# Two stages of a decoder layer in seven products instead of eight: the query projection of cross-attention, and the first two column blocks of the feed-forward

## The chip, the cores and the metric

The kernel runs on one core of a Trainium2 chip. Its time is the device time of one execution in microseconds; a figure for a kernel is the median of several executions. The engines are named as in the profile: PE (TensorE matmul) with its weight loads (PEld), DVE (VectorE), ACT (ScalarE), POOL (GpSimd) and SP (SyncE, which issues the DMAs).

## The reference, cut to what matters

One decoder layer over 1024 tokens of width 1024: a token mixer (stick-breaking attention and a Mamba-2 mixer side by side), cross-attention into 256 memory tokens with 4 heads, and a SwiGLU feed-forward with 2816 hidden units. Each part takes a normalised input and adds its normalised output to the stream. The change touches the second and the third part:

```python
x = x + rms_norm(merged @ w_mix_out[l], g_post_mix[l])
h = rms_norm(x, g_pre_xa[l])
mem_n = rms_norm(mem, g_mem[l])
x = x + rms_norm(memory_cross_attention(h, mem_n, w_xq[l], w_xkv[l], w_xo[l]), g_post_xa[l])
h = rms_norm(x, g_pre_ffn[l])
x = x + rms_norm(swiglu(h, w_gu[l], w_down[l]), g_post_ffn[l])
```

Inside, `q = h @ w_xq`, then scores, softmax and `o @ w_xo`; the feed-forward is `(silu(h @ w_gate) * (h @ w_up)) @ w_down`. All numbers are fp32.

## The kernel before, in words

**Products in two parts.** An fp32 matrix is held as a high part (rounded to fp32r, a form that PE multiplies fast) and a low part, the rest. `hi_sb` makes the high part as a copy on ACT or POOL, `lo_of` (L101) the low part as a subtraction, mostly on DVE. A product is then three matmuls per block of 128 rows of the inner dimension (`mm3`, L104 to L106, or `acc3`, L215 to L217): high by high, high by low, low by high. A matmul of one weight block of 128x128 with 512 columns is written 128x512 in the profile.

**Seven products instead of eight.** A product of two matrices that are cut into 2x2 blocks needs eight block products, or seven after Winograd and Strassen, if sums and differences of blocks are made first. Here the inner dimension (1024) is cut in two, the tokens are cut in two halves of 512, and two column blocks of the weight form a pair. `winograd_weights` (L173) makes the sums s1 to s4 of the weight's quarters on POOL (L183 to L186) and splits all seven; `winograd_pair` (L222) does the seven products of 12 matmuls each. On the other side stand the blocks b11, b21 (first half of the tokens) and b22, and the combinations t1 to t4 of the halves. The plain way takes 8 x 12 matmuls for a pair.

**The order of the stages.** `out_proj` (L1398) multiplies by an output matrix, chunk by chunk of 128 tokens (48 matmuls each, four chunks a call), then adds the normalised result to the stream (L1414 square and sum on ACT, `rstd_of` on POOL, L1416 and L1417 on DVE), stores it, and calls `pre_norm` (L157), which normalises the stream for the next part (L160 ACT, L161 DVE), transposes it (8 transposes, L165) and splits it into high (L166, ACT) and low (L167, DVE). After both halves (`hx`), the query projection follows: `proj` (L1443) for 8 column blocks and 2 halves, each 24 matmuls. The first two blocks' products with the first half stand ahead (`pre`, L1467): they need only tokens that are finished, while the last chunk is still being normalised. `wq_load` (L1434) loads a weight block and splits it.

Then come the scores (`soft`, L1506), softmax, transposes of prob (`turn_`, L1520) and the mix with the values (`mix`). The output matrix of cross-attention is loaded and split by `big_weight` (L1329, 8 slices of 512 KB through two raw buffers); its buffers lie on the right side of the memory, where qT and part of prob were. A second pair of `out_proj` calls follows.

**The feed-forward's beginning.** The first two of its 22 column blocks (a gate block and an up block each) are done the plain way by `standard` (192 matmuls). Beside them `combos` forms t1, t2 and t3 from the split blocks: `whole` (L1601) adds the high and the low part again, L1610 to L1614 subtract, `split` makes high and low; t4 follows after both (L1626). Only then come the 20 pairs of `strassen`.

**What sets the order.** A scheduler places the instructions of each engine in one fixed order when the kernel is built; an engine then waits at each instruction for what it needs. `behind(marks[n])` makes some loads and splits come after a named instruction. Pools hold a set number of buffers, and a new tile waits for the last reader of the buffer that it takes over.

## Time and profile before

| | us |
|---|---|
| median of 3 runs | 2554.7 (2552.59 to 2555.76) |
| profiled execution | 2557.21 |
| its span | 2555.4 |
| PE busy in the span | 2475.9 (97%) |
| DVE, ACT, POOL busy | 1772.8, 1133.7, 853.9 |
| query projection | 1638.4 to 1730.0 in the span |
| attention's scores, softmax and mix | 1730.0 to 1792.9 |
| second output projection | 1792.9 to 1887.9 |
| plain feed-forward blocks | 1887.9 to 1934.3 |
| the 20 pairs | 1934.3 to 2324.3 |

A row of a timeline reads: start in us from the span's start, length in us, engine, line, operation, output and inputs by the program's names, shape, number of instructions; in brackets the idle time before it and what ended it. Where rows overlap on PE, the matmuls run through the array one behind the other, and the distance of two starts is what one costs. The mean granted clock of PE was 0.992 of full speed in this execution.

### The profile page before, as it was taken

Reading aid. Unit: us, or ns where it says so; the run is one execution under the profiler, and the core shown is the slowest. Engines: PE = TensorE matmul, PEld = TensorE weight load, DVE = VectorE, ACT = ScalarE, POOL = GpSimd, SP = SyncE. Lnnn points to the kernel's source line nnn. Section 1 sums busy time; section 2 is a strip of 40 time slices with the busy share of each in tenths; the row PEclk is TensorE's granted clock in tenths of the full one; section 3 lists DMA queues with packets and bytes.
Section 4 is the critical chain, followed back from the end, with each engine's and each line's share of the span. In section 5 each row is a group of like instructions: output and inputs, shape, how many; then the busy total and the mean of one; then the engine's idle time right before and its main releaser. Section 6 shows DMA issues by size and latency. Waiting matters only on the chain. (4 is left out here: it accounts for less than half of the span.)

```text
span 2555.4 us, 33383 instructions
## 1 busy us (share of the span) xinstructions
PE 2475.9 (97%) x12378; PEld 2033.6 (80%) x12378; DVE 1772.8 (69%) x2093; ACT 1133.7 (44%) x2023; POOL 853.9 (33%) x650
## 2 busy tenths in 40 slices
PE   7999999999999999999999999999999999999998
PEld 5788888887888878777777788887787888888876
DVE  7665777767578787688888664316459666666997
ACT  5333455555456665566554213215233333334343
POOL 3221544443121211256656040101113333323772
PEclk9999999999999999999999999999999999999999
DMA  7431443332543434365332662311232232224232
GB/s 246 152 116 55 138 149 99 99 112 90 153 112 87 120 99 104 100 207 168 107 106 65 203 209 83 124 50 34 99 116 66 83 91 75 90 91 165 99 132 99
DMA packets 255275, 293.51 MB, mean 115 GB/s; under 512 B 17023, under 2 KB 175240, under 8 KB 254986
## 3 DMA queue, kind: packets, MB, share of 16 engines
q1 hardware_dynamic: 255114, 291.40, 36.6%
q8 instruction: 97, 1.59, 0.3%
q14 instruction: 64, 0.52, 0.1%
HBM read 200.10 MB, written 74.45 MB: 107 GB/s over the span
## 5 line engine op out<-in xcount | busy, mean ns | idle before, releaser
L875 DVE TENSOR_TENSOR_SCAN n<-n,mask 128x128 f32<-128x128 f32 (+7 forms) x128 | 181.7, 1445 | 23.4 <-ACT n L874 22.2
L101 DVE TENSOR_TENSOR sw<-sf,sw 128x512 fp32r<-128x512 f32 x150 | 120.9, 818 | 82.0 <-ACT sw L98 80.5
L892 ACT ACTIVATE wth<-tr,mone 128x512 fp32r<-128x512 f32 x192 | 110.2, 584 | 81.4 <-PE tr L889 80.6
L98 ACT ACTIVATE sw<-sf 128x512 fp32r<-128x512 f32 x150 | 92.1, 626 | 113.0 <-PE mm L217 97.8
L183 POOL TENSOR_TENSOR sf<-wr,wr 128x512 f32<-128x512 f32 x38 | 59.4, 1563 | 233.4 <-DMA wr<-in_w_gu_dram 116.7
L893 DVE SCALAR_TENSOR_TENSOR wtl<-tr,wth 128x512 fp32r<-128x512 f32 x192 | 99.3, 544 | 53.9 <-ACT wth L892 53.8
L98 ACT ACTIVATE sw<-wr 128x512 fp32r<-128x512 f32 x113 | 71.2, 631 | 126.2 <-PE mm L217 125.6
L217 PE MATMUL mm<-h,sw 128*128 128x512 f32 x320 | 125.0, 392 | 1.8 <-DVE sw L101 1.8
L215 PE MATMUL mm<-h,sw 128*128 128x512 f32 x320 | 122.6, 391 | 2.9 <-ACT h L98 2.3
L216 PE MATMUL mm<-h,sw 128*128 128x512 f32 x320 | 125.3, 391 | 0.0
L101 DVE TENSOR_TENSOR sw<-wr,sw 128x512 fp32r<-128x512 f32 x113 | 106.6, 945 | 21.1 <-ACT sw L98 21.0
L669 DVE SCALAR_TENSOR_TENSOR b<-b,prmT,b 128x1023 f32<-128x1023 f32 (+2 forms) x72 | 109.6, 1522 | 15.1 <-ACT b L667 14.5
L94 POOL TENSOR_SCALAR v<-va 128x512 fp32r<-128x512 f32 x16 | 20.6, 1289 | 278.2 <-PE av L902 164.0
L874 ACT ACTIVATE n<-sc 128x512 f32<-128x512 f32 (+1 forms) x192 | 88.6, 494 | 45.5 <-PE tr L889 28.8
L152 POOL TENSOR_SCALAR rstd<-ms 128x1 f32<-128x1 f32 x74 | 28.1, 379 | 237.1 <-ACT x L1414 110.3
L104 PE MATMUL mm<-oth,bw 128*128 128x512 f32 x256 | 103.6, 405 | 3.6 <-DVE a L1214 3.6
L104 PE MATMUL p<-bw,h 128*128 128x512 f32 x256 | 98.7, 391 | 3.3 <-DVE x L1416 2.4
L105 PE MATMUL mm<-otl,bw 128*128 128x512 f32 x256 | 100.5, 393 | 0.0
L106 PE MATMUL mm<-oth,bw 128*128 128x512 f32 x256 | 100.4, 392 | 0.0
L106 PE MATMUL p<-bw,h 128*128 128x512 f32 x256 | 100.1, 392 | 0.0
L105 PE MATMUL p<-bw,h 128*128 128x512 f32 x256 | 99.9, 390 | 0.0
L185 POOL TENSOR_TENSOR sf<-wr 128x512 f32<-128x512 f32 x38 | 63.0, 1657 | 105.4 <-DVE sw L101 105.4
(616 smaller groups left out, 8044.0 us busy)
## 6 DMA issues: line engine op xcount, KB each, us to landing
wr<-in_w_gu_dram SPq DMA_DIRECT2D x80, 256.0 KB
wr<-in_w_in_dram SPq DMA_DIRECT2D x36, 512.0 KB
zr<-in_w_in_dram SPq DMA_DIRECT2D x28, 512.0 KB
gu_d<-t SPq DMA_DIRECT2D x44, 256.0 KB
wraw<-in_w_in_dram SPq DMA_DIRECT2D x20, 512.0 KB
zs_d<-zo SPq DMA_DIRECT2D x32, 256.0 KB
xs_d<-b SPq DMA_DIRECT2D x32, 256.0 KB
kl<-gt SPq DMA_DIRECT2D x64, 128.0 KB
```

Source lines behind the costliest of these rows:

```text
L98: A.activation(o, i, AF.Copy)
L101: eng.tensor_tensor(o, i, hi.bitcast(F32), ALU.subtract)
L104: first = T.matmul(ps, sh, mh, start=start, stop=False)
L105: T.matmul(ps, sh, ml, start=False, stop=False)
L106: T.matmul(ps, sl, mh, start=False, stop=stop)
L215: T.matmul(ps, w[0][:, k, :], bh, start=first and k == 0, stop=False, skip_group_check=True)
L216: T.matmul(ps, w[0][:, k, :], bl, start=False, stop=False, skip_group_check=True)
L217: ins = T.matmul(ps, w[1][:, k, :], bh, start=False, stop=last and k == 3, skip_group_check=True)
L669: V.scalar_tensor_tensor(acc[:, sh:], y[:, :S - sh], cw(3 - sh, f), acc[:, sh:], ALU.mult, ALU.add)
L875: V.tensor_tensor_scan(nt[:, 0:L][:, ::-1], nt[:, 0:L][:, ::-1], mask[:, S - L:][:, ::-1], 1.0, ALU.mult, ALU.max)
L892: A.activation(wh[:, t0 * P:], pt[:, t0 * P:], AF.Identity, bias=mone)
L893: V.scalar_tensor_tensor(wl[:, t0 * P:], pt[:, t0 * P:], -1.0, wh[:, t0 * P:].bitcast(F32), ALU.add, ALU.subtract)
```

## The change

- The query projection is done in four pairs of seven products. Two pairs are interleaved in a new function `two_pairs`, the other two go through `winograd_weights` and `winograd_pair`. The same `two_pairs` does the first two column blocks of the feed-forward; `standard`, `combos`, `whole` and the t4 loop are gone.
- The combinations are formed in fp32 straight from the transposes, before a split. In the first half each chunk is also copied to fp32 tiles (x11 and x21, two more ACT copies); in the second half `pre_norm` forms b22, t1 and the fp32 block of t2 chunk by chunk (L1462, L1464 to L1466 in the new file). `other_blocks` then makes t3 and t4 (four subtractions of 128x1024, L1484 and L1487) and splits t2, t3 and t4 (six high parts on ACT, six low parts on DVE).
- Ahead of the last chunk stand three products (`lead_products`, 36 matmuls) in place of two `proj` calls (48), with weights from `lead_weights`.
- In `two_pairs`, s1 is made on DVE (L1526), s2, s3 and s4 on POOL. The raw weights are loaded into tiles that are used later for other things: qT4 to qT7 in the query projection, fg and fw in the feed-forward.
- Memory: the values and the transposed keys take over the fp32 tiles; the pools of prob and of the softmax parts now lie where `big_weight`'s raw buffers and first slices come to lie, and qT lies beyond them. The keys' load is issued later. The reservation for software DMA is 256 instead of 1024.

The diff, cut to its core (the bodies of the removed functions stand above):

```diff
-    def pre_norm(psp, xt, yt, gbc, outs):
+    def pre_norm(psp, xt, yt, gbc, put):
 
         ms = mk(stats, [P, 1], F32, "ms")
         A.activation(yt, xt, AF.Square, scale=D ** -0.5, accum_out=ms)
         V.scalar_tensor_tensor(yt, xt, rstd_of(ms), gbc, ALU.mult, ALU.mult)
-        for kh, (hi, lo) in enumerate(outs):
-            pt = mk(psp, [P, 4, P], F32, "tr")
+        pts = []
+        for kh in range(2):
+            pts.append(mk(psp, [P, 4, P], F32, "tr"))
             for k in range(4):
-                T.transpose(pt[:, k, :], yt[:, (kh * 4 + k) * P:(kh * 4 + k + 1) * P], ident)
-            A.activation(hi, pt, AF.Copy)
-            V.tensor_tensor(lo, pt, hi.bitcast(F32), ALU.subtract)
+                T.transpose(pts[kh][:, k, :], yt[:, (kh * 4 + k) * P:(kh * 4 + k + 1) * P], ident)
+        put(pts, yt)
...
+        r0 = mk(rawp, [P, 4, 2, P], F32, tag)
+        r1 = mk(rawp, [P, 4, 2, P], F32, tag)
...
+            both[i] = mk(firstp if firstp is not None and i in (0, 3) else swp, [P, 2, 4, P], F32R, "sw")
...
     h2 = pool(px, "h2", 8)
-    wq = pool(px, "wq", 2)
+    xk = pool(px, "xk", 1)
+    ld = pool(px, "ld", 2)
     xt4 = ExitStack()
     t4 = pool(xt4, "t4x", 3)
+    psa = pool(px, "psa", 2, PSUM)
...
-    def wq_load(rawp, tag, src, rb=None, eng=None):
...
+    def fp32_blocks():
+
+        return [mk(xk, [P, 4, HALF], F32, f"xk{i}") for i in range(3)]
+
+    def first_half(hb, xf):
+        hb["b11"], hb["b21"] = quad(accp, "a8")
+
+        def at(cs):
+            def put(pts, yt):
+                for nm, pt in zip(("b11", "b21"), pts):
+                    hi, lo = [t[:, :, cs] for t in hb[nm]]
+                    A.activation(hi, pt, AF.Copy)
+                    V.tensor_tensor(lo, pt, hi.bitcast(F32), ALU.subtract)
+                for x, pt in zip(xf, pts):
+                    A.activation(x[:, :, cs], pt, AF.Copy)
+            return put
+        return at
+
+    def second_half(hb, xf):
+        hb["b22"], hb["t1"] = quad(h2, "h2")
+
+        def at(cs):
+            def put(pts, yt):
+                b22, t1 = [[t[:, :, cs] for t in hb[nm]] for nm in ("b22", "t1")]
+                x = yt[:, 0:HALF].rearrange("p (k t) -> p k t", t=P)
+                A.activation(b22[0], pts[1], AF.Copy)
+                V.tensor_tensor(x, pts[0], xf[0][:, :, cs], ALU.subtract)
+                A.activation(t1[0], x, AF.Copy)
+                V.tensor_tensor(b22[1], pts[1], b22[0].bitcast(F32), ALU.subtract)
+                V.tensor_tensor(xf[2][:, :, cs], pts[1], x, ALU.subtract)
+                V.tensor_tensor(t1[1], x, t1[0].bitcast(F32), ALU.subtract)
+            return put
+        return at
+
+    def other_blocks(hb, xf, tx):
+
+        hb["t2"], hb["t3"] = quad(h2, "h2")
+        hb["t4"] = tuple(mk(tx, [P, 4, HALF], F32R, "tx") for _ in range(2))
+        x11, x21, x2 = xf
+
+        def split(x, nm):
+            hi, lo = hb[nm]
+            for k in (0, 2):
+                hi_sb(hi[:, k:k + 2, :], x[:, k:k + 2, :], "a")
+                lo_of(lo[:, k:k + 2, :], x[:, k:k + 2, :], hi[:, k:k + 2, :])
+
+        split(x2, "t2")
+        for k in (0, 2):
+            V.tensor_tensor(x11[:, k:k + 2, :], x2[:, k:k + 2, :], x11[:, k:k + 2, :], ALU.subtract)
+        split(x11, "t3")
+        for k in (0, 2):
+            V.tensor_tensor(x21[:, k:k + 2, :], x21[:, k:k + 2, :], x2[:, k:k + 2, :], ALU.subtract)
+        split(x21, "t4")
+
+    def quarter_load(dst, w, kh, c0):
+        nc.sync.dma_start(dst.rearrange("p k b f -> p k (b f)"), w[kh * 512:(kh + 1) * 512, c0:c0 + 2 * P].rearrange("(k p) f -> p k f", p=P))
+
+    def split_weight(pl, tag, x):
+        o = mk(pl, [P, 2, 4, P], F32R, tag)
+        hi_sb(o[:, 0], x, "a")
+        lo_of(o[:, 1], x, o[:, 0])
+        return o[:, 0], o[:, 1]
+
+    def lead_weights(wbig, w):
+
+        raws = [mk(wbig, [P, 4, 2, P], F32, "wraw", 2) for _ in range(2)]
+        for kh in range(2):
+            quarter_load(raws[kh], w, kh, 0)
+        return [split_weight(pl, tag, raws[kh][:, :, p]) for pl, tag, kh, p in ((ld, "sw", 0, 0), (ld, "sw", 1, 0), (t4, "x4", 0, 1))]
+
+    def lead_products(hb, lead, pa, pb):
+        acc3(pa[0], lead[0], hb["b11"], True, False)
+        acc3(pb[0], lead[1], hb["b21"], True, True)
+        acc3(pa[1], lead[2], hb["b11"], True, False)
+
+    def two_pairs(hb, pa, pb, pc, raws, w, c1, sfp, swp, y, last, blocks):
+
+        (a11, a12), (a21, a22) = raws
+        for r, kh, c0 in ((a12, 1, 0), (a21, 0, c1), (a22, 1, c1), (a11, 0, 0)):
+            quarter_load(r, w, kh, c0)
+        acc3(pb[1], split_weight(swp, "sw", a12[:, :, 1]), hb["b21"], True, True)
+        for p in range(2):
+            A.activation(y[p][0][0], pa[p], AF.Copy)
+            V.tensor_tensor(y[p][0][0], y[p][0][0], pb[p], ALU.add)
+
+        def pick(r):
+            return [r[:, :, p] for p in range(2)]
+
+        def combined(eng, dst, x, z, op):
+            for o, i, j in zip(dst, x, z):
+                eng.tensor_tensor(o, i, j, op)
+            return dst
+
+        def rooms():
+            return [mk(sfp, [P, 4, P], F32, "sf") for _ in range(2)]
+
+        def weights(x):
+            return [split_weight(swp, "sw", t) for t in x]
+
+        def products(ps, ws, nm, start, stop, then):
+            for p in range(2):
+                acc3(ps[p], ws[p], hb[nm], start, stop)
+                then(p)
+
+        a11, a12, a21, a22 = [pick(r) for r in (a11, a12, a21, a22)]
+        s1 = combined(V, rooms(), a21, a22, ALU.add)
+        w1 = weights(s1)
+        s2 = combined(G, rooms(), s1, a11, ALU.subtract)
+        blocks()
+        w2 = weights(s2)
+        products(pc, w1, "t1", True, False, lambda p: A.activation(y[p][1][1], pc[p], AF.Copy))
+        w4 = weights(combined(G, a12, a12, s2, ALU.subtract))
+        products(pa, w2, "t2", False, False, lambda p: A.activation(y[p][0][1], pa[p], AF.Copy))
+        w3 = weights(combined(G, a21, a11, a21, ALU.subtract))
+        products(pc, w4, "b22", False, True, lambda p: V.tensor_tensor(y[p][0][1], y[p][0][1], pc[p], ALU.add))
+        w7 = weights(a22)
+        products(pa, w3, "t3", False, False, lambda p: V.tensor_tensor(y[p][1][1], y[p][1][1], pa[p], ALU.add))
+        products(pa, w7, "t4", False, True, lambda p: last(p, pa[p]))
...
-        hx = [quad(accp, "a8")]
-        out_proj(0, mg[0], wmix, t4, psp, x_in, x2_d, gpost, gpre, hx[0])
-        hx.append(quad(h2, "h2"))
-        out_proj(1, mg[1], wmix, t4, psp, x_in, x2_d, gpost, gpre, hx[1])
+        hx = {}
+        xf = fp32_blocks()
+        out_proj(0, mg[0], wmix, t4, psp, x_in, x2_d, gpost, gpre, first_half(hx, xf))
+        out_proj(1, mg[1], wmix, t4, psp, x_in, x2_d, gpost, gpre, second_half(hx, xf))
         with behind(marks[AFTER_M]):
-            wqs = [wq_load(wbig, "wraw", colblock(a["w_xq"][0], f * P), 2, "a") for f in range(2)]
-    pre = [proj(wqs[f], hx[0]) for f in range(2)]
+            lead = lead_weights(wbig, a["w_xq"][0])
+
+    def bank():
+        return mk(psa, [P, HALF], F32, "mm")
+
+    def two_banks():
+        t = mk(psp, [P, 2, HALF], F32, "p2")
+        return t[:, 0], t[:, 1]
+
+    w_xq = a["w_xq"][0]
+    b0, b1 = bank(), bank()
+    b2, b3 = two_banks()
+    lead_products(hx, lead, (b0, b2), (b1, b3))
     x1.close()
 
     with ExitStack() as q2:
+        qp = pool(q2, "qp", side="right")
+        qT = [mk(qp, [P, S], F32, f"qT{f}") for f in range(KT)]
+
+        def halves_of(f):
+            return [qT[f][:, 0:HALF], qT[f][:, HALF:S]]
+
+        def fourth(f, ps):
+            A.activation(qT[f][:, 0:HALF], ps, AF.Copy)
+
+        with ExitStack() as xs:
+            sfp = pool(xs, "qsf", 4, side="right")
+            swp = pool(xs, "qsw", 6, side="right")
+            tx = pool(xs, "qtx", 2, side="right")
+            raws = [[qT[4 + 2 * b + kh].rearrange("p (k b f) -> p k b f", k=4, b=2) for kh in range(2)] for b in range(2)]
+            two_pairs(hx, (b0, b2), (b1, b3), two_banks(), raws, w_xq, 2 * P, sfp, swp,
+                      [[halves_of(p), halves_of(2 + p)] for p in range(2)], lambda p, ps: fourth(2 + p, ps), lambda: other_blocks(hx, xf, tx))
+            for f in (4, 6):
+                def loads(r, kh):
+                    yield r.rearrange("p k b f -> p k (b f)"), w_xq[kh * 512:(kh + 1) * 512, f * P:(f + 2) * P].rearrange("(k p) f -> p k f", p=P)
+
+                ws = winograd_weights(t4, sfp, swp, loads, 0, "x4", ld)
+                fourth(f + 1, winograd_pair(None, ws, hx, [halves_of(f), halves_of(f + 1)], None, two_banks() + (bank(),)))
...
-        qp = pool(q2, "qp", side="right")
-        kp = pool(q2, "kp", side="right")
-        qT = [mk(qp, [P, S], F32, f"qT{f}") for f in range(KT)]
-        kT = mk(kp, [P, KT, ML], F32, "kT")
+        kT = mk(xk, [P, KT, ML], F32, "xk2")
         vh, vl = [], []
         nc.sync.dma_start(kT, kT_d)
-        for f in range(2):
-            A.activation(qT[f][:, 0:HALF], pre[f], AF.Copy)
-        for f in range(KT):
-            w = wqs[f] if f < 2 else wq_load(t4, "x4", colblock(a["w_xq"][0], f * P))
-            for half in range(2):
-                if f < 2 and half == 0:
-                    continue
-                pq = proj(w, hx[half])
-                A.activation(qT[f][:, half * HALF:(half + 1) * HALF], pq, AF.Copy)
         for m in range(2):
             t = mk(t4, [P, D], F32, "x4")
             nc.sync.dma_start(t, vx_d[m * P:(m + 1) * P, :])
-            vh.append(mk(wq, [P, D], F32R, "qhi"))
-            vl.append(mk(wq, [P, D], F32R, "qlo"))
+            v = mk(xk, [P, 2, D], F32R, f"xk{m}")
+            vh.append(v[:, 0])
+            vl.append(v[:, 1])
...
-        hf = [quad(accp, "a8")]
-        out_proj(0, ox[0], wxo, t4, psp, x2_d, x3_d, gpost, gpre, hf[0])
-        hf.append(quad(h2, "h2"))
-        out_proj(1, ox[1], wxo, t4, psp, x2_d, x3_d, gpost, gpre, hf[1])
+        hw = {}
+        xf = fp32_blocks()
+        out_proj(0, ox[0], wxo, t4, psp, x2_d, x3_d, gpost, gpre, first_half(hw, xf))
+        out_proj(1, ox[1], wxo, t4, psp, x2_d, x3_d, gpost, gpre, second_half(hw, xf))
         with behind(marks[NCH + AFTER_O]):
-            wgu = [wq_load(wbig, "wraw", colblock(a["w_gu"][0], c0), 2, "a") for c0 in (0, FFN)]
-        pre = [proj(w, hf[0]) for w in wgu]
+            lead = lead_weights(wbig, a["w_gu"][0])
+    psx.close()
+    psf = pool(px, "psf", 6, PSUM)
+
+    def fbank():
+        return mk(psf, [P, HALF], F32, "mm")
+
+    pa_, pb_ = (bank(), fbank()), (bank(), fbank())
+    lead_products(hw, lead, pa_, pb_)
     xt4.close()
...
-        def standard(f):
...
+        def results():
+            return [[mk(t2, [P, HALF], F32, "t2"), mk(t2, [P, HALF], F32, "t2")], [None, mk(t2, [P, HALF], F32, "t2")]]
+
+        raws = [mk(fdp, [P, 2, S], F32, nm) for nm in ("fg", "fw")]
+        raws = [[t[:, kh].rearrange("p (k b f) -> p k b f", k=4, b=2) for kh in range(2)] for t in raws]
+        y = [results() for _ in range(NLEAD)]
+        sgs = []
+
+        def both_gated(f, ps):
+            if not sgs:
+                t = mk(xk, [P, 4, HALF], F32, "xk0")
+                sgs.extend(t[:, i] for i in range(4))
+            gated(f, 0, y[f][0][0], ps, sgs[2 * f])
+            gated(f, 1, y[f][0][1], y[f][1][1], sgs[2 * f + 1])
+
+        two_pairs(hw, pa_, pb_, (fbank(), fbank()), raws, w_gu, FFN, sfp, swp, y, both_gated, lambda: other_blocks(hw, xf, tx))
```

80 lines of the change are left out of this document (14 added, 66 removed).

## The prediction

> **What bounds the kernel now.** I read the page first: the span, the busy line and the row of the granted clock.
>
> ```profile
> span 2555.4 us, 33383 instructions
> PE 2475.9 (97%) x12378; PEld 2033.6 (80%) x12378; DVE 1772.8 (69%) x2093; ACT 1133.7 (44%) x2023; POOL 853.9 (33%) x650
> PEclk9999999999999999999999999999999999999999
> ```
>
> PE has work for 97% of the span, at nearly full clock. So the time is the number of matmuls times their spacing, plus the few places where PE stands still. The spacing is not the mean of one matmul: the timeline of PE shows it from start to start, here where the feed-forward's pairs begin (L215 to L217, one product is 12 of them) and stall.
>
> ```profile
> 1934.28 0.39 PE L215 MATMUL mm<-a,sw 128*128 128x512 f32 x1
> 1934.50 0.39 PE L216 MATMUL mm<-a,sw 128*128 128x512 f32 x1
> 1938.81 0.39 PE L217 MATMUL mm<-h,sw 128*128 128x512 f32 x1
> 1941.51 0.50 PE L215 MATMUL mm<-h,sw 128*128 128x512 f32 x1 [2.31 <-ACT h L98]
> 1943.34 0.63 PE L217 MATMUL mm<-a,sw 128*128 128x512 f32 x1
> 1943.76 0.63 PE L215 MATMUL mm<-a,sw 128*128 128x512 f32 x1
> 1952.27 0.50 PE L217 MATMUL mm<-h,sw 128*128 128x512 f32 x1 [1.80 <-DVE sw L101]
> ```
>
> From 1934.28 to 1938.81 lie 20 spacings, 0.2267 us each, though each row says 0.39: the matmuls overlap. After a stall some follow at 0.42. Next the two stages that the change rewrites, with the table of stretches (length, then busy time of PE, PEld, DVE, ACT and POOL with instructions, clock, DMA share, GB/s):
>
> ```profile
> 1638.40:1729.70 91.30, 91.30 (x412) 75.81 (x411) 14.86 (x14) 16.25 (x26) 5.79 (x8) 1.00 0.22 70
> 1729.70:1792.85 63.15, 58.59 (x279) 48.34 (x278) 42.73 (x64) 33.64 (x97) 8.73 (x5) 0.95 0.10 34
> 1887.90:1934.30 46.40, 45.93 (x210) 37.74 (x210) 35.87 (x40) 15.37 (x26) 16.35 (x13) 1.00 0.27 85
> 1934.00:1945.00 11.00, 8.69 (x33) 6.72 (x33) 11.00 (x20) 4.92 (x9) 0.00 (x0) 0.89 0.10 29
> 1945.00:1957.00 12.00, 10.05 (x34) 7.39 (x33) 12.00 (x21) 4.64 (x8) 4.70 (x1) 0.81 0.26 87
> 1957.00:1980.00 23.00, 23.00 (x103) 19.04 (x102) 17.99 (x23) 11.15 (x21) 10.04 (x7) 1.00 0.22 69
> 1980.00:2320.00 340.00, 340.00 (x1502) 281.53 (x1501) 214.30 (x248) 122.33 (x211) 102.02 (x65) 1.00 0.27 84
> ```
>
> The query projection (first row) never stops PE, and DVE has 15 us of work in 91. The feed-forward's two plain column blocks (1887.9 to 1934.3) lose 46.40 - 45.93 = 0.47 us. Then DVE is busy for all of 1934 to 1957, making the combinations that the pairs need, and PE waits. From 1957 on nothing is lost: 340 us hold 1502 matmuls, 0.2264 each. The 23 us from 1934 to 1957 hold some 64 to 67 matmuls where there was room for 101, so 7.8 to 8.5 us are lost there; I take 8.4, half of it waiting and half matmuls at half the clock (0.89 and 0.81 in the rows).
>
> **The change, part by part.**
>
> *Matmuls.* By the code, the query's 384 (8 column blocks, 2 halves, 24) become 4 pairs x 7 products x 12 = 336, and the first two feed-forward blocks go from 192 to 168. 72 fewer at 0.2267 us: **-16.3 us**, certain since PE is the limit there. The old feed-forward stalls, 8.4 + 0.47, go with the code that made them: **-8.9 us**. What replaces them is the question.
>
> *The query's combinations.* Before, the last chunk of the output projection was hidden like this (DVE, and POOL's rstd in the brackets):
>
> ```profile
> 1638.42 0.39 PE L104 MATMUL mm<-a,qhi 128*128 128x512 f32 x1
> 1640.74 1.28 DVE L1416 SCALAR_TENSOR_TENSOR x<-p,rstd,g_post_mix 128x1024 f32<-128x1024 f32 x1 [3.04 <-POOL rstd L153]
> 1642.05 1.23 DVE L1417 TENSOR_TENSOR x<-x,x 128x1024 f32<-128x1024 f32 x1
> 1643.20 1.28 DVE L167 TENSOR_TENSOR h<-tr,h 128x512 fp32r<-128x512 f32 x2
> 1645.46 1.28 DVE L161 SCALAR_TENSOR_TENSOR x<-x,rstd,g_pre_xa 128x1024 f32<-128x1024 f32 x1 [0.98 <-POOL rstd L153]
> 1949.73 0.68 DVE L1626 TENSOR_TENSOR t<-t,t 128x512 f32<-128x512 f32 x1
> 1950.34 0.68 DVE L1601 TENSOR_TENSOR t<-a,a 128x512 f32<-128x512 f32 x1
> 1899.72 1.03 PE L165 MATMUL tr<-ident,x 128*128 128x128 f32 x8
> ```
>
> A DVE operation costs its spacing: 1.15 us for 128x1024 (1642.05 to 1643.20), 0.60 for 128x512 (1949.73 to 1950.34). Eight transposes cost PE some 0.9. Before, 48 plain matmuls (10.9 us) stood on PE ahead of the last chunk's half, and hundreds that needed only finished halves behind them. Now only three products, 36 matmuls (8.2 us), plus the a12 product, need the first half alone. Everything after needs t1 to t4, which need the last chunk, and DVE makes them in one fixed order. The changed program's DVE order behind L161 of the last chunk (its end 1645.46 + 1.28, and 0.60 more for a subtraction put in front: 1647.3) is: the third lead weight's low half; after the transposes (0.5 wait) L1462, L1519, L1464, L1465, L1466; four 128x1024 subtractions (L1484, L1487); a weight's low half; two t2 low halves; a12's low half; a t3 half; two s1 sums; the other t3 half; two t4 halves; one more weight's low half, for which PE's fixed order waits before the first t1 product. That is 10 x 1.15 + 11 x 0.60 + 0.5 = 18.6 us, so 1665.9. In front of that point PE has 54 matmuls and 16 transposes, 12.24 + 1.8 = 14.0 us from 1638.4: done at 1652.4. **PE stands still for 13.5 us**, in several pieces. Behind it a product takes 2.72 us of PE against 0.6 to 1.2 of DVE: PE is the limit again.
>
> That is with DVE at its best pace. POOL now forms s2, s3 and s4 from 1662 on, and beside POOL the same operations are slow:
>
> ```profile
> 1913.93 2.32 DVE L101 TENSOR_TENSOR qlo<-wr,qhi 128x1024 fp32r<-128x1024 f32 x1
> 1916.17 3.48 DVE L101 TENSOR_TENSOR h<-t,h 128x512 fp32r<-128x512 f32 x2
> 1913.44 1.73 POOL L183 TENSOR_TENSOR sf<-wr,wr 128x512 f32<-128x512 f32 x1 [5.28 <-DMA wr<-in_w_gu_dram]
> 1952.30 5.91 POOL L183 TENSOR_TENSOR sf<-wr,wr 128x512 f32<-128x512 f32 x1 [19.28 <-DVE sw L101]
> ```
>
> With POOL at work DVE took 2.32 where 1.23 is usual and 1.74 instead of 0.68; in another place DVE went on at 0.60 and POOL's took 5.91. Three wide and two narrow operations at risk: 3 x 1.09 + 2 x 1.06 = 5.4 more, 18.9 at worst. I take **+15** for the query, bounds 13.5 and 18.9. The Trainium skill, page "SBUF — State Buffer", section "Who interferes with whom", says that a VectorE operation with two SBUF inputs and a GpSimd operation that reads SBUF exclude each other for their whole length, the first to issue winning. By that rule either row is possible, and the sum is one of the two bounds, not the middle; the 5.91 agrees, the doubled DVE times only partly.
>
> *The loads.* What a load takes is seen at the first weights of cross-attention's output projection, on SP and on POOL, which starts when the first has landed:
>
> ```profile
> 1759.28 37.71 SPq L1333 DMA_DIRECT2D wraw<-in_w_xo_dram  x6
> 1762.94 1.05 POOL L94 TENSOR_SCALAR bw<-wraw 128x1024 fp32r<-128x1024 f32 x1 [42.79 <-DMA wraw<-in_w_xo_dram]
> ```
>
> The raw weights of the second products are queued on SP behind the last chunk's x2 store and a load whose buffer L161 frees, so they issue at about 1647.5. A load of 512 KB takes 3.7 us; if the five needed first overlap somewhat they are there from 1651 to 1659 (an estimate, 3.7 for the first and about 1.5 to 2 for each further one), before the DVE order gets to them. I cost them at nothing; if they came 3 us later than that, s1 and the stall would be 3 us later.
>
> *The feed-forward's combinations.* The same chain, from these rows:
>
> ```profile
> 1887.94 0.39 PE L104 MATMUL mm<-a,qhi 128*128 128x512 f32 x1
> 1895.15 1.28 DVE L161 SCALAR_TENSOR_TENSOR x<-x,rstd,g_pre_ffn 128x1024 f32<-128x1024 f32 x1
> ```
>
> L161 of the last chunk ends 8.5 us after the lead's start, 9.1 with the extra subtraction. Behind it: 4.0 (lo, wait, five), 4.6 (four subtractions), 0.6 (a12), 2.3 (t2), 1.2 (s1), 4.6 (t3, t4), 0.6 (L1519), 0.6 (s1's low half): 27.6. PE has 56 matmuls and 16 transposes, 14.5 us, in front of it: **13.1 us still**, and 4 x 1.09 + 2 x 1.06 = 6.5 more beside POOL, 19.6. I take **+15** here too.
>
> *The half clock.* Each long stall is followed by some eight matmuls 0.2 us slower (1943.34 to 1943.76), 1.6 us. Two stalls make 3.2; most fall where DVE sets the pace anyway. I take **+1**, bounds 0 and 3.2.
>
> *The output weights of cross-attention.* Their buffers now lie where prob and the softmax tiles lie, so their loads (those of 1759.28) wait for the last transposes of attention. The rest of the rows that this concerns:
>
> ```profile
> 1764.07 2.39 POOL L101 TENSOR_TENSOR bw<-wraw,bw 128x1024 fp32r<-128x1024 f32 x1
> 1786.15 1.03 PE L1520 MATMUL tr<-ident,prob 128*128 128x128 f32 x8
> 1792.85 0.61 PE L104 MATMUL p<-bw,h 128*128 128x512 f32 x2
> 1769.14 1.91 DVE L1512 TENSOR_TENSOR prob<-prob,sm 128x1024 f32<-128x1024 f32 x1
> 1771.78 1.26 DVE L1512 TENSOR_TENSOR prob<-prob,sm 128x1024 f32<-128x1024 f32 x1
> 1771.20 0.30 PE L1520 MATMUL tr<-ident,prob 128*128 128x128 f32 x1 [1.49 <-ACT prob L1510]
> ```
>
> The first loads were issued 33 us before the projection began. Now the last transposes end 5.9 us before its first matmul; 3.7 for the load, 1.05 and 2.39 for the split give 7.1, so the first low half comes 1.2 late, and the following slices come through two raw buffers a little slower than PE uses them (12 matmuls, 2.72 us each). I take **+3.4**, bounds 1.2 and 6. In return POOL no longer works beside attention's softmax (1.91 of DVE against 1.26 when POOL is done) ahead of the 1.49 us gap: **-1**, bounds -4.5 (all of that stretch's 63.15 - 58.59 idle time) and +2 (the first scores now start behind the projection's last copies).
>
> *At nothing:* the extra ACT copies and DVE operations of each chunk in the two output projections (four of 0.60 in place of two, two copies) and the moved gain and key loads, hidden under the 48 matmuls, 10.9 us, of the next chunk; for the last chunk they are in the chain above. Uncovered they would cost about 2 us a chunk.
>
> **Sum:** -16.3 - 8.9 + 15 + 15 + 1 + 3.4 - 1 = **+8.2 us**. The profiled execution took 2557.2 (span 2555.4 and 1.8 around it) and would take 2565.4; it is 2.5 above the median, so on the median 2554.7 I forecast **2563 us**. Differences under 0.2% (5 us) are about what a measurement can't tell from none.
>
> **Rivals.**
> 1. *DVE keeps its pace and POOL waits.* Stalls 13.5 and 13.1, weights 1.2, attention -1, clock 0: -25.2 + 26.8 + 1 = about +2, 2556. The 5.91 of POOL speaks for it, the 2.32 and 3.48 of DVE against. Same: 0.2.
> 2. *Faster: the chain doesn't pass in single file.* If the low halves of the lead weights, t1 and a12 are done while PE is on the lead, and the wide subtractions overlap with what PE can still do, PE stands still for less. The point where the sign turns: both stalls together 25.2 - 3.4 (clock, weights, attention as above) = 21.8, that is 10.9 each. With 6 each: -25.2 + 12 + 3.4 = -9.8, 2545. For it: DVE has 15 us of work in the 91 of the old projection, so it starts with empty hands. Against it: DVE's order is fixed, and its first link is L161 of the last chunk, 8.9 us after the lead's start. 0.2.
> 3. *Contention at its worst in both chains*: -25.2 + 18.9 + 19.6 + 1 + 3.4 - 1 = +16.7, 2571; with the weights and the clock at their upper bounds too, 2576. The rows at 1913 to 1920 speak for it; that they show one stretch only, against. 0.15.
>
> That leaves 0.45 for my forecast. The range takes in the rivals: **2545 to 2575**, and leaves out little but the corners. Faster by over 0.2% 0.2, within 0.2, slower 0.6.
>
> **What would show it.** In the new profile: 336 and 168 + 1680 product matmuls; PE idle of 13 to 19 us within 30 us of the first query product, released by DVE's low halves (L101), with DVE busy throughout; the same at the feed-forward's lead; nothing lost between the second feed-forward pair and the end of the pairs; a wait on the output weights (bw) at the second output projection. It is wrong if these stalls are under 9 us each, or if PE waits for DMA there instead, since then the queue and not DVE would be the limit.

## The result and the profile after

| | before | after |
|---|---|---|
| median, us | 2555.23 (4 runs, 2552.59 to 2559.07) | 2572.38 (4 runs, 2570.50 to 2573.42) |
| ratio | | 1.0061, 95% interval 1.0049 to 1.0074 |
| profiled execution, us | 2557.21 | 2570.50 |

The changed kernel is slower, by 17 us on the medians and 13.4 us between the two profiled spans. From the page of the changed kernel, the span, the busy line and the granted clock:

```profile
span 2568.8 us, 33386 instructions
PE 2464.2 (96%) x12306; PEld 2019.2 (79%) x12306; DVE 1815.4 (71%) x2129; ACT 1165.5 (45%) x2075; POOL 880.3 (34%) x666
PEclk9999999999999999999999999899999999999999
```

PE has 72 instructions fewer (12378 before) and the span is still longer: PE stands still more, and in one of the 40 slices the granted clock has fallen to 8. The table of stretches of the changed kernel (length, then busy time of PE, PEld, DVE, ACT and POOL with instructions, clock, DMA share, GB/s) shows where:

```profile
1639.24:1735.85 96.61, 84.44 (x354) 68.17 (x353) 54.49 (x64) 34.66 (x56) 29.10 (x19) 0.91 0.23 80
1735.85:1797.39 61.54, 58.48 (x289) 48.64 (x288) 40.67 (x63) 32.63 (x96) 1.95 (x2) 1.00 0.10 35
1797.39:1895.62 98.23, 94.39 (x433) 76.48 (x432) 45.53 (x47) 31.95 (x54) 19.54 (x34) 1.00 0.34 118
1895.62:1927.33 31.71, 18.84 (x71) 13.65 (x69) 28.22 (x31) 17.01 (x25) 12.17 (x8) 0.82 0.41 132
1927.33:1950.00 22.67, 22.67 (x89) 18.58 (x90) 20.29 (x19) 9.89 (x17) 13.99 (x9) 0.88 0.08 24
1950.00:2320.00 370.00, 370.00 (x1634) 306.39 (x1633) 235.13 (x275) 136.37 (x234) 113.93 (x74) 1.00 0.28 86
```

The rows are the query projection, attention, the second output projection, and three parts of the feed-forward. In the query PE is busy for 84.44 of 96.61 us, where before it never stopped; at the feed-forward's lead it is busy for 18.84 of 31.71. From 1950 to 2320 nothing is lost: 1634 matmuls in 370 us, 0.2264 each.

The next table goes by the first matmul of each stage on PE's timeline; "lost" is the length less 0.2267 us a matmul and 0.11 a transpose. The 91.5 us of the old query stage (1638.42 on) hold 12 of attention's score matmuls, 2.7 us, which are put to attention here.

| us | before | after | difference | forecast |
|---|---|---|---|---|
| up to the query | 1638.4 | 1639.2 | +0.8 | 0 |
| query projection | 88.8 | 96.6 | +7.8 = -10.9 (matmuls) + 18.7 (lost) | -10.9 + 15, and half of +1 |
| attention | 65.6 | 61.6 | -4.1 | -1 |
| second output projection | 95.1 | 98.2 | +3.1 | +3.4 |
| feed-forward | 436.4 | 441.9 | +5.5 = -5.4 (matmuls) - 10.3 (old losses) + 21.2 (lost) | -5.4 - 8.9 + 15, and half of +1 |
| the rest | 231.1 | 231.3 | +0.2 | 0 |

The waits of PE in the two stretches (what waited and for what; us, times, longest), the query first:

```profile
PE mm L215 <- ACT sw L98: 8.6, 2, 6.5
PE p L215 <- ACT sw L98: 1.4, 1, 1.4
PE p L215 <- ACT x L98: 1.4, 1, 1.4
PE tr L166 <- DVE x L161: 0.8, 1, 0.8
```

and the feed-forward's:

```profile
PE mm L215 <- ACT sw L98: 6.6, 2, 4.4
PE mm L217 <- DVE sw L101: 3.3, 1, 3.3
PE tr L166 <- DVE x L161: 2.8, 1, 2.8
```

The wait is not one stall but five pieces and four, and most of it is put down not to DVE but to ACT's copies of weights (L98). What ACT waited for is a step further back. Here is DVE in the changed kernel's query, start and length in us:

```profile
1647.17 1.29 DVE L161 SCALAR_TENSOR_TENSOR x<-x,rstd,g_pre_xa 128x1024 f32<-128x1024 f32 x1 [0.77 <-POOL rstd L153]
...
1652.27 2.35 DVE L1484 TENSOR_TENSOR xk<-xk,xk 128x1024 f32<-128x1024 f32 x2
1654.54 2.35 DVE L1487 TENSOR_TENSOR xk<-xk,xk 128x1024 f32<-128x1024 f32 x2
...
1661.42 1.28 DVE L1526 TENSOR_TENSOR sf<-qT,qT 128x512 f32<-128x512 f32 x2
...
1663.76 2.35 DVE L101 TENSOR_TENSOR tx<-xk,tx 128x1024 fp32r<-128x1024 f32 x2
...
1666.63 1.29 DVE L101 TENSOR_TENSOR sw<-sf,sw 128x512 fp32r<-128x512 f32 x2
```

DVE works at its full pace, 1.14 us a wide operation, and comes to s1's low halves at 1666.63. POOL forms s2 meanwhile, and ACT and PE wait for it:

```profile
1662.24 6.80 POOL L1526 TENSOR_TENSOR sf<-sf,qT 128x512 f32<-128x512 f32 x1 [15.10 <-DVE sf L1526]
1669.00 1.27 POOL L1526 TENSOR_TENSOR qT<-qT,qT 128x512 f32<-128x512 f32 x1
...
1917.13 6.14 POOL L1526 TENSOR_TENSOR sf<-sf,fg 128x512 f32<-128x512 f32 x1 [13.65 <-DVE sf L1526]
```

```profile
1669.07 0.63 ACT L98 ACTIVATE sw<-sf 128x512 fp32r<-128x512 f32 x1 [5.70 <-POOL sf L1526]
```

```profile
1669.76 0.67 PE L215 MATMUL mm<-h,sw 128*128 128x512 f32 x1 [2.08 <-ACT sw L98]
...
1927.33 0.80 PE L215 MATMUL mm<-h,sw 128*128 128x512 f32 x1 [2.13 <-ACT sw L98]
1927.92 0.63 PE L216 MATMUL mm<-h,sw 128*128 128x512 f32 x1
1928.35 0.63 PE L217 MATMUL mm<-h,sw 128*128 128x512 f32 x1
```

An operation that takes POOL 1.27 us while DVE stands still (so the changed kernel's rows at 1669.00 and 1671.92) took 6.80 and 6.14 beside DVE's row of operations. In the query it ended 1.1 us after DVE's run of subtractions (1667.92 and 1669.04). In the feed-forward DVE ran on, and POOL's operation ended 1.2 us after DVE had begun one that reads a matmul result (`mm`):

```profile
1922.06 0.68 DVE L1519 TENSOR_TENSOR t<-t,mm 128x512 f32<-128x512 f32 x1
```

ACT copies s2's high half a moment later, PE goes on 0.7 us after that, and the matmuls behind the wait come 0.43 us apart (1927.92 to 1928.35), not 0.2267.

### The profile page after: what moved, and what is told of

Its sections match the earlier page's. It is cut to its first block, busy times and chain, and to the rows that moved or that the text cites. A ratio compares the mean times of both kernels' runs of the same rounds, so it can differ in the third digit from the quotient of the medians.

```text
span 2568.8 us, 33386 instructions
## 1 busy us (share of the span) xinstructions
PE 2464.2 (96%) x12306; PEld 2019.2 (79%) x12306; DVE 1815.4 (71%) x2129; ACT 1165.5 (45%) x2075; POOL 880.3 (34%) x666
## 5 line engine op out<-in xcount | busy, mean ns | idle before, releaser
L875 DVE TENSOR_TENSOR_SCAN n<-n,mask 128x128 f32<-128x128 f32 (+7 forms) x128 | 188.4, 1497 | 23.4 <-ACT n L874 22.2
L101 DVE TENSOR_TENSOR sw<-sf,sw 128x512 fp32r<-128x512 f32 x166 | 135.7, 830 | 92.5 <-ACT sw L98 90.4
L98 ACT ACTIVATE sw<-sf 128x512 fp32r<-128x512 f32 x166 | 102.4, 627 | 159.1 <-PE mm L217 120.3
L215 PE MATMUL mm<-h,sw 128*128 128x512 f32 x360 | 142.5, 396 | 8.8 <-ACT sw L98 8.7
L216 PE MATMUL mm<-h,sw 128*128 128x512 f32 x360 | 141.7, 394 | 0.0
L217 PE MATMUL mm<-h,sw 128*128 128x512 f32 x360 | 138.1, 392 | 0.0
L101 DVE TENSOR_TENSOR sw<-wr,sw 128x512 fp32r<-128x512 f32 x113 | 108.8, 964 | 29.9 <-ACT sw L98 29.7
L183 POOL TENSOR_TENSOR sf<-wr,wr 128x512 f32<-128x512 f32 x38 | 53.1, 1399 | 217.9 <-DMA wr<-in_w_gu_dram 145.8
L98 ACT ACTIVATE sw<-wr 128x512 fp32r<-128x512 f32 x113 | 71.2, 631 | 116.4 <-PE mm L217 115.6
L105 PE MATMUL p<-bw,h 128*128 128x512 f32 x256 | 100.5, 393 | 1.5 <-POOL bw L101 1.4
L105 PE MATMUL mm<-otl,bw 128*128 128x512 f32 x256 | 100.5, 393 | 0.0
L106 PE MATMUL mm<-oth,bw 128*128 128x512 f32 x256 | 100.4, 392 | 0.0
```

The costliest lines, as they stand in the source:

```text
L98: A.activation(o, i, AF.Copy)
L101: eng.tensor_tensor(o, i, hi.bitcast(F32), ALU.subtract)
L105: T.matmul(ps, sh, ml, start=False, stop=False)
L106: T.matmul(ps, sl, mh, start=False, stop=stop)
L215: T.matmul(ps, w[0][:, k, :], bh, start=first and k == 0, stop=False, skip_group_check=True)
L216: T.matmul(ps, w[0][:, k, :], bl, start=False, stop=False, skip_group_check=True)
```

## The experiments

**Theory A:** DVE's single file sets the end; PE stands still until DVE has made t2, t3 and t4 for the half and s1 for the weights, in the order that the code gives. **Rival B:** late loads, since the longest wait (6.52 us, at 1662.24) is for a weight copied as soon as its DMA landed. It is a weight of the third pair, with which PE's fixed order goes on in this place:

```profile
1661.55 0.63 ACT L98 ACTIVATE sw<-x 128x512 fp32r<-128x512 f32 x1 [2.83 <-DMA x<-in_w_xq_dram]
1662.24 0.80 PE L215 MATMUL mm<-a,sw 128*128 128x512 f32 x1 [6.52 <-ACT sw L98]
```

**Rival C:** DVE and POOL hinder each other. (In the expectation of e1 the same letter stands for the half clock.) Lengths of the stages in all runs, read like the table above (the query of before with its 12 score matmuls taken out):

| kernel | ratio to before, 95% | query | second output projection | feed-forward |
|---|---|---|---|---|
| before | 1 | 88.8 | 95.1 | 436.4 |
| after | 1.0061 (1.0049 to 1.0074) | 96.6 | 98.2 | 441.9 |
| e1_lows_out | 1.0000 (0.9991 to 1.0010) | 91.0 | 100.0 | 433.1 |
| e2_loads_first | 1.0049 (1.0034 to 1.0064) | 98.2 | 98.2 | 441.9 |
| e3_s2_on_dve | 1.0036 (1.0022 to 1.0051) | 92.7 | 98.6 | 441.8 |
| e4_s1_first | 1.0031 (1.0021 to 1.0042) | 97.0 | 98.2 | 437.3 |
| e5_reordered | 0.9981 (0.9973 to 0.9989) | 87.1 | 100.4 | 428.4 |
| e6_pool_s3_s4 | 1.0001 (0.9991 to 1.0012) | 88.7 | 98.5 | 433.2 |
| e7_all_s_on_dve | 1.0048 (1.0031 to 1.0064) | 95.4 | 98.4 | 439.2 |
| e8_wxo_off_pool | 0.9984 (0.9974 to 0.9994) | 88.0 | 100.5 | 431.2 |
| e9_early_wxo | 0.9954 (0.9938 to 0.9970) | 87.0 | 94.1 | 430.8 |
| e10_warm_lead | 0.9982 (0.9972 to 0.9992) | 87.6 | 100.4 | 431.3 |
| e11_early_and_warm | 0.9966 (0.9954 to 0.9979) | 87.6 | 93.9 | 432.4 |

Each length is from one profiled execution. Stages whose code is the same differ by 1 to 4 us from profile to profile (the feed-forward of e5 and e8 to e11: 428.4 to 432.4), and the start of the query, behind untouched code, lies between 1633.4 and 1639.4. A difference under 4 us in the feed-forward, or under 2 us in another stage, decides nothing.

### e1_lows_out: less in DVE's file

```diff
             for k in (0, 2):
                 hi_sb(hi[:, k:k + 2, :], x[:, k:k + 2, :], "a")
-                lo_of(lo[:, k:k + 2, :], x[:, k:k + 2, :], hi[:, k:k + 2, :])
+            hb[nm] = hi, hi
```

> The low halves of t2, t3 and t4 are left out in both stages (the high half stands in for them), so six 128x1024 subtractions of 1.13 us go from DVE's chain in each; the matmuls stay as many. Theory A, DVE's single file sets both stalls: the changed kernel becomes 12 to 15 us faster (about 2558), the s2 wait behind the chain (2.1 us in each stage) goes too, because POOL is let in earlier; the query stalls then end with the load of the second weight of the third pair. Rival B, the raw-weight loads set the stalls: at most 3 us in the query and nothing to speak of in the feed-forward, where the loads were there early. Rival C, the half clock after long waits costs most: the waits shrink, but the slow matmuls stay, gain under 6 us.

Measured 2556.85 beside 2556.35 of before, 15.6 us under the changed kernel by the ratios (0.0061 of 2556); query -5.6, feed-forward -8.7. As theory A had it: six subtractions of 1.14 us less in each stage's file, and PE gets that time back. The half clock as the main cost falls, since it would have given under 6 us. It isn't the whole of the loss, since waits on DVE remain at the feed-forward's lead:

```profile
PE mm L217 <- DVE sw L101: 3.6, 2, 3.1
```

### e2_loads_first: the raw weights earlier

The loads of the third pair are put behind those of the first two on SP, so that the weights that two_pairs needs come first.

```diff
-                ws = winograd_weights(t4, sfp, swp, loads, 0, "x4", ld)
+                with tc.issue_after(quarters[-1].ins):
+                    ws = winograd_weights(t4, sfp, swp, loads, 0, "x4", ld)
```

> Only the order on SP is changed: the four raw loads of the first two query pairs are issued ahead of the loads of the third and fourth pair, so some 4 us earlier. Theory A (DVE's chain): the low half of s1 comes at the same time, within 1 us; the wait of 6.52 us that the profile puts down to a weight's high half only changes its name, the sum of the query's waits stays, total within 1.5 us of the changed kernel. Rival B (loads): the query's stalls shrink by 4 us or more, total -4 to -6.

Measured 2570.1, by the ratios 3 us under the changed kernel with intervals that overlap, and the query 1.6 us longer, not shorter. The 6.52 us wait is gone, and two others stand in its place:

```profile
PE mm L215 <- ACT sw L98: 7.1, 1, 7.1
...
PE p L217 <- DVE sw L101: 4.0, 1, 4.0
```

s2 on POOL started earlier and took the longer for it, since DVE's run still had to end:

```profile
1659.61 8.54 POOL L1528 TENSOR_TENSOR sf<-sf,qT 128x512 f32<-128x512 f32 x1 [13.90 <-DVE sf L1528]
```

```profile
1657.00 1.13 ACT L98 ACTIVATE sw<-x 128x512 fp32r<-128x512 f32 x2
...
1668.17 0.63 ACT L98 ACTIVATE sw<-sf 128x512 fp32r<-128x512 f32 x1 [7.43 <-POOL sf L1528]
```

Rival B falls: in the changed kernel the load was the last to come, but what stood behind it was late by as much. Here ACT copies the third pair's weights at 1657.00 without a wait, and PE stands until 1668.86 all the same, for s2.

### e3_s2_on_dve: s2 away from POOL

```diff
-        s2 = combined(G, rooms(), s1, a11, ALU.subtract)
+        s2 = combined(V, rooms(), s1, a11, ALU.subtract)
```

> s2 is formed on DVE (two 128x512 operations of 0.60 per stage) in place of POOL, whose first s2 took 6.80 and 6.14 us in the changed kernel. Theory A with POOL starved by DVE's run: the t1 weights come 0 to 1.2 us later, but the wait of about 2.1 us for s2's high half goes in both stages, and less half clock follows: -2 to -4 us. Rival: POOL's length is an artefact and s2 is not what PE waits for: +2 us, from the two more operations on DVE in each stage.

Measured 2567.07, 6.4 us under the changed kernel by the ratios, more than expected. The query is 3.9 us shorter, the feed-forward as long as it was (441.8). So without POOL's starved s2 the query loses some 4 us less; in the feed-forward no gain shows: PE waits 2.8, 3.5, 5.2 and 1.4 us there, with DVE's file two operations longer. So the profile shows the gain in one of the two stages only.

### e4_s1_first: the order alone

The block combinations (`blocks()`: t2, t3, t4) are placed behind s1's low halves, so that DVE first makes what PE can use.

```diff
         s2 = combined(G, rooms(), s1, a11, ALU.subtract)
-        blocks()
+        with tc.issue_after(lows[-1].ins):
+            blocks()
```

> Only DVE's order is changed: the operations on t2, t3 and t4 come behind the low halves of s1's weights in both stages; nothing is added. If the position in DVE's file were all, a12 and s1 would come 4.6 to 10 us earlier in the feed-forward and the total would fall by 8 to 10 us. If POOL is kept out as long as DVE runs without a break, s2 is still late, PE waits there instead, and the total falls by 2 to 4 us only; in the query next to nothing, since s1 waits for its loads until about 1657.

Measured 2564.71, 7.7 us under the changed kernel by the ratios and so between the two expectations; the feed-forward is 4.6 us shorter, the query not. Here POOL got in right behind a short pause of DVE (1906.90 to 1907.00), and from then on the two went turn by turn. DVE, then POOL, at the feed-forward's lead:

```profile
1909.31 4.54 DVE L101 TENSOR_TENSOR h<-xk,h 128x1024 fp32r<-128x1024 f32 x2
1913.77 2.31 DVE L1484 TENSOR_TENSOR xk<-xk,xk 128x1024 f32<-128x1024 f32 x1
```

```profile
1907.10 3.43 POOL L1531 TENSOR_TENSOR sf<-sf,fg 128x512 f32<-128x512 f32 x2 [7.38 <-DMA fg<-in_w_gu_dram]
1910.50 4.50 POOL L1531 TENSOR_TENSOR fw<-fg,fw 128x512 f32<-128x512 f32 x2
```

A wide DVE operation took 2.3 us instead of 1.14, POOL's 2.25 instead of 1.27. So the order alone helps less than it could, since POOL works beside it; rival C has a part.

### e5_reordered: order, combinations and loads together

```diff
-        s2 = combined(G, rooms(), s1, a11, ALU.subtract)
-        blocks()
+        s2 = combined(V, rooms(), s1, a11, ALU.subtract)
         w2 = weights(s2)
+        with tc.issue_after(lows[-1].ins):
+            blocks()
...
-        w4 = weights(combined(G, a12, a12, s2, ALU.subtract))
+        w4 = weights(combined(V, a12, a12, s2, ALU.subtract))
...
-        w3 = weights(combined(G, a21, a11, a21, ALU.subtract))
+        w3 = weights(combined(V, a21, a11, a21, ALU.subtract))
```

and the edit of e2.

> All orders turned at once, no computation left out: on SP the raw loads of the first two query pairs ahead of those of the other two; on DVE the weights of s1 and s2 ahead of t2, t3 and t4; s2, s3 and s4 on DVE instead of POOL. Theory A (what PE waits for is the place of a12, s1 and s2 in DVE's single file, and POOL shut out by it): PE needs a12 some 4 us after its lead and then has 24 matmuls (5.4 us) for every 1.2 to 3 us of DVE, so the waits of 12.2 us in the query and 13.4 in the feed-forward fall to 4 to 6 each. Query stage 96.6 to 87 to 90, feed-forward 441.9 to 427 to 431, total 18 to 24 us under the changed kernel, that is 2549 to 2555, level with the kernel before or a little under it. Rival: DVE's whole work in the stretch (some 19 us) is the bound in whatever order; then no more than e1's 15 us less work would give, and in fact under 8 us.

Measured 2550.46 (12 runs) beside 2556.9: faster than before, 20 us under the changed kernel. The query, with its stretch below, and the feed-forward (428.4) came out where they were expected.

```profile
1637.69:1724.74 87.05, 82.80 (x353) 66.57 (x352) 57.43 (x70) 34.53 (x56) 15.08 (x13) 0.96 0.26 88
```

```profile
PE p L215 <- ACT x L98: 1.3, 1, 1.3
PE mm L216 <- DVE h L101: 0.9, 1, 0.9
PE tr L166 <- DVE x L161: 0.8, 1, 0.8
```

DVE has more work in this query than the changed kernel gave it (57.43 us, 54.49 there), and PE waits for 4 us instead of 12 (three short waits of 1.3 us together are not among the rows). So the amount of DVE's work does not by itself set the loss: what it does first does, and that s2, s3 and s4 are not made by POOL beside it. The earlier loads are part of this kernel too, and no run has the rest of it without them.

### e6_pool_s3_s4 and e7_all_s_on_dve: which of the edits

e6 is e5 with s3 and s4 back on POOL (`combined(G, ...)` for w4 and w3); e7 is e5 without the new order and without the earlier loads, so that only the engine of s2, s3 and s4 is changed.

> As e5, but s3 and s4 stay on POOL (s2 on DVE). If DVE and POOL shut each other out operation by operation, as e4's feed-forward shows (2.31 for 1.22, 1.73 for 0.68), the four POOL operations of 1.7 either double DVE's times or come late: 2 to 6 us slower than e5. If the two only slow each other where one runs without a break, no difference from e5 beyond 1 us.

> s2, s3 and s4 on DVE in the changed kernel's order, nothing else. Against e3 (s2 alone on DVE) four more operations of 0.60 come into DVE's file but nothing of these stages is left to POOL except the next pair's sums. By the single file: within 2 us of e3, that is 3 to 8 us under the changed kernel. If contention were the main cost of the changed kernel: 8 us or more under it.

e6: 2556.9, 6.4 us slower than e5; in the stages that is +4.7 and +1.7, but kernels with e5's feed-forward differ by 4.0 there, so where it falls isn't decided. e7: 2565.56, feed-forward 439.2, query 95.4. So without the order, taking POOL away brings little (1.0048 against the changed kernel's 1.0061, within the intervals); with the order, s3 and s4 alone are worth 6 us. The order alone (e4) gives 7.7 us by the ratios, the engine alone (e7) 3.3, and the two with the earlier loads 20. Neither does it alone. The feed-forward, whose loads are the same in all of these, shows it without the loads: 441.9, with the order 437.3, with DVE for s2 to s4 439.2, with both 428.4 (430.8 to 432.4 in the later kernels that share this code).

### e8_wxo_off_pool and e9_early_wxo: the second output projection

In the changed kernel the projection's weights are late: SP issues their loads at 1791.74, PE starts on them at 1797.39 and waits for slices that POOL splits.

```profile
1791.74 13.45 SPq L1333 DMA_DIRECT2D wraw<-in_w_xo_dram  x5
```

```profile
1798.93 0.50 PE L105 MATMUL p<-bw,h 128*128 128x512 f32 x1 [0.93 <-POOL bw L101]
```

e8 (e5, and no slice split on POOL) asks whether POOL is the slow part; e9 (e5, and the first two raw slices loaded into buffers that are free during attention) whether it is the load:

```diff
-        wxo = big_weight(wbig, a["w_xo"][0], 2)
+        wxo = big_weight(wbig, a["w_xo"][0], 0)         (e8)
+        wxo = big_weight(wbig, a["w_xo"][0], 2, t4)     (e9)
...
-            raw = mk(wb, [P, D], F32, "wraw", bufs=2)
+            raw = mk(wb, [P, D], F32, "wraw", bufs=2) if early is None or k > 1 else mk(early, [P, D], F32, "x4")
```

> As e5, and the first two slices of cross-attention's output weights are split by ACT and DVE alone, not by POOL (whose low half takes 2.39 us against 1.2 on DVE). If the split sets the pace at the start of the second output projection: that stage falls from 98.2 us by 1 to 2.5, total as much under e5. If the late load alone does (it is issued only when attention's last transposes are done): under 0.5 us.

> As e5, but the raw tiles of the first two slices of cross-attention's output weights lie in the stream's tiles, which are free during attention, so that these two loads are issued before the last transposes; the split still waits for them. If the late load, and then the two raw buffers that each wait for the split before (about 6.3 us for two slices where PE takes 5.4), make the second output projection 98.2 to 100.4 us long: it falls to 95 to 97, total 2 to 5 us under e5. If the split's destination (under prob) is what counts: under 1 us.

e8: 2551.81, the stage 100.5 against 100.4 in e5. POOL's pace is not it. e9: **2543.55** beside 2557.0 of before, by the ratios 7 us under e5 where 2 to 5 were expected, and the stage takes 94.1 us, even 1 less than before the change. SP issues the second of the two early slices 94 us ahead of the use, and the first 97 matmuls run without a gap:

```profile
1692.28 0.33 SPq L1333 DMA_DIRECT2D x<-in_w_xo_dram  x1
...
1760.42 37.37 SPq L1333 DMA_DIRECT2D wraw<-in_w_xo_dram  x6
```

```profile
1786.44:1808.60 22.16, 22.14 (x97) 17.75 (x95) 8.66 (x9) 4.78 (x6) 5.10 (x6) 1.00 0.36 118
```

So in e5 the late load costs this stage some 6 us. In the changed kernel, where the stage is 3.1 us longer than before, it was not tried alone; why it is longer still in e5 (100.4 against 98.2) stays open. e9 beats both kernels. 3.3 of the 13.9 us between its profiled span (2541.5) and that of before lie ahead of the query, in untouched code; the stages from the query on account for some 10.

### e10_warm_lead and e11_early_and_warm: keeping PE busy in a short wait

In e5 eight matmuls behind the two short waits of the query ran at half rate. Eight matmuls whose result is overwritten are put ahead of the third lead product in the query, to keep the clock up; e10 is e5 with them, e11 is e9 with them.

```diff
         acc3(pb[0], lead[1], hb["b21"], True, True)
+        for k in range(4 if hb is hx else 0):
+            for h in range(2):
+                T.matmul(pa[1], lead[1][h][:, k, :], hb["b21"][0][:, k, :], start=True, stop=False, skip_group_check=True)
         acc3(pa[1], lead[2], hb["b11"], True, False)
```

> As e5, and eight matmuls without use are put on PE in the query's lead, between the second and the third product, where PE waits 1.3 us; they write a bank that the third product starts anew, so the result is the same. In e5 eight matmuls behind these waits (1.34 and 0.75 us) took 0.427 in place of 0.227. If short waits bring the half clock: these eight are back at 0.227 and the query's stage is 0.5 to 1.8 us shorter (some of it may be given back at DVE's next wait). If not: 0 to 0.5 us longer.

> e9 and e10 together, as the best version: the sum of their gains, 2 to 6 us under e5, that is 2544 to 2549 against some 2556 of the kernel before in the same call (0.995 to 0.9975).

e10: 2552.44, query 87.6 against 87.1: no gain. The matmuls behind the gap do come 0.23 us apart there, and PE gives the time back at later waits (4.9 us of standing still in the query, 4.3 in e5). e11: 2547.6, in the range that was expected, but not better than e9 (0.9966 and 0.9954, intervals that overlap). That the extra matmuls kept the clock up isn't shown: in e9, without them, the half rate had not come in the first place, as the last section shows.

## Why the prediction was right and where it was wrong

The forecast was 2563 us, 8.2 more than before, in a range of 2545 to 2575. Measured were 2572.4 us, 17.2 more: inside the range, near its upper end, and about twice the change that was forecast.

**Right.** The sign and the cause: single file on DVE in front of products that need the last chunk (e1, e5). The matmuls (72 fewer by the page) and the old stalls (10.3 us by the count of lost time, 8.9 forecast). The path up to s1's low half: forecast 1665.9 in the query from a lead at 1638.4, found to start at 1666.63 with its first half done some 0.65 later, from a lead at 1639.24; in the feed-forward 27.6 us behind the lead, found from here:

```profile
1922.65 2.84 DVE L101 TENSOR_TENSOR sw<-sf,sw 128x512 fp32r<-128x512 f32 x2
```

that is 27.0 to its start. Up to that point PE has lost 14.7 us in the query and 14.8 in the feed-forward (lengths 28.3 and 28.4, 52 matmuls and 16 transposes each), where the forecast had 15 and 15. That match is in part luck. The forecast was 13.5 and 13.1 at DVE's best pace and 1.5 and 1.9 more for a DVE slowed by POOL, and up to here DVE was not slowed; the rest came from an end 0.8 us later and from two and four matmuls fewer ahead of it. Nor did PE wait for s1 at this point: its longest wait was for the third pair's weight in the query (6.52 us) and already for s2 in the feed-forward (4.45 us, ended by the ACT copy that POOL released at 1923.30). The late output weights came as forecast (+3.1 for +3.4); e9 shows in e5 that the load is their cause. And loads at nothing, by e2: where they came earlier the stage was no shorter, although PE did wait on one.

**Wrong.** The step that failed is the sentence behind the query's chain: "Behind it a product takes 2.72 us of PE against 0.6 to 1.2 of DVE: PE is the limit again", and with it the half clock at +1. Behind s1's low half another 4.0 us are lost in the query (18.7 in all) and 6.4 in the feed-forward (21.2). The losses are these, by the same count:

| lost, us | up to s1's low half | to the end of the wait for s2 | in all |
|---|---|---|---|
| query | 14.7 (by 1667.5) | 17.0 (by 1669.76) | 18.7 |
| feed-forward | 14.8 (by 1923.98) | 17.7 (by 1927.33) | 21.2 |

The middle part, 2.3 and 2.9 us, is the wait for s2, which PE's fixed order puts right behind the first matmuls with s1 and which POOL could not finish in time beside DVE's run. I had POOL's 5.91 among my rows, and weighed only what POOL does to DVE (2.32 for 1.23), as if a waiting POOL were free. Rival 1 has the mechanism of the query and the first part of the feed-forward's lead (DVE keeps its pace, POOL waits), and its price of 2556 is wrong for the same reason. (Its sum also has a +1 that its list lacks: 13.5 + 13.1 + 1.2 - 1 is 26.8, and -25.2 + 26.8 is +1.6, still 2556.) Rival 3's price, 2571, is the nearest to what was measured, but by luck: it comes from a DVE slowed throughout both chains. The last part is mostly half clock: behind the wait for s2 come nine and thirteen spacings of 0.3 to 0.6 us, 1.7 and 2.7 us more than at 0.2267 a piece. In the whole of the two stretches, with the idle time taken out, there are 34 and 31 such spacings, 6.6 and 6.7 us too long, against "some eight" behind each of two stalls. The stall came in five pieces and in four, and each piece can start such a row. Some of these fell where DVE set the pace anyway and cost nothing (e5 and e9 have 4.3 and 6.8 us of standing still in the query, 4.9 and 2.3 of slow spacing, and the same length); behind s1 they cost up to their whole size.

**Sizes that went the other way.** Attention gave 4.1 us and not 1, and most of that is chance. PE's waits there fell from 4.5 to 2.8 us, near the forecast; the rest is half rate that came before and not in this profile (granted clock 0.95 and 1.00): the 96 matmuls with the values took 25.7 us and then 23.1. In e4, with the same attention code, they took 24.7, and attention 63.2 instead of 61.6. POOL has almost nothing beside the softmax (1.95 us busy in the stretch of the changed kernel, 8.73 before); that the shorter waits come from POOL's absence was not tried. Together: both chains 8.9 us more than forecast (39.9 lost for 31), attention 3.1 and the old losses 1.4 less, the rest (start, output weights, end) +0.7; that is 5.1 us, and the difference of the spans is 13.4 where 8.2 were forecast. The medians lie 17 apart, 3.8 more than the profiled pair; this is within what single executions differ by, and no cause was looked for.

**What the profile was to show.** PE idle of 13 to 19 us in each stage, released by DVE's L101: it was 12.2 and 13.4, and put down to ACT's L98 for 11.4 us in the query and 6.6 in the feed-forward. The sign given for being wrong, PE waiting for DMA, seemed to be there (6.52 us at 1662.24, one step back), and by its own sign the prediction would have been wrong; but e2 moved the loads and the loss stayed: what a wait is put down to is the last of several that were late together.

**Rule and row.** The Trainium skill, page "SBUF — State Buffer", section "Who interferes with whom", has a DVE operation with two SBUF inputs and a POOL operation that reads SBUF exclude each other for an instruction's length, the first to issue winning. The turns in e4 (2.27 for 1.14, with POOL's 2.25) agree. That a waiting POOL operation gets no turn for 6.14 to 8.54 us, over several ends of DVE operations, the rule as stated doesn't give; the measurement decides.

**Open.** Why POOL and DVE go on turn by turn once POOL has got in, while a POOL operation that arrives during DVE's run starves (seen: it gets in behind a pause of DVE or at an operation that reads a matmul result); why the second output projection is 2 us longer in e5; whether e11's extra matmuls cost anything beside e9.

## What to carry to other kernels

When a stage is rewritten so that fewer matmuls need more prepared operands, write down the order in which the preparing engine delivers them beside the order in which PE uses them: the loss was in what came first (s1 behind t2, t3 and t4), and most of it went when the order was changed and the second engine's part given to DVE, with more work on DVE and not less. An operand that a second engine makes beside a busy DVE belongs in that list with the time it takes there (6 us for 1.3), up to the last operand that PE needs in a row and not only the first. And before a load is called the cause because the last wait names it, move the load and see whether another wait of the same size appears.
